# Memory queries as two more units of the gates, and the memory's norm inside u's second half

## The chip, the cores and the metric

The kernel runs on one core of a Trainium2 chip. The metric is the device time of one execution in microseconds (us); the time before is the median of 3 runs.

## The reference, cut to what matters

One decoder layer: a half-step SwiGLU, a mixing block with three branches, a second half-step SwiGLU. The mixing block has one input projection, whose columns feed everything in it:

```python
h = rmsnorm(x, mix_norm)                 # x: 1024 tokens x 1024
z = h @ w_in                             # [u | v | c_q | c_kv | k_rope | q_mem | gate_A | gate_B | gate_C]
u, v = gelu(z_u), gelu(z_v)              # 512 wide each
y_a = spatial_gating(u, v, ...)          # u * (tril(W_s) layernorm(v) + b) in chunks of 128
y_b = mla(...)                           # causal attention with low-rank q and kv
def memory_attention(q_m, mem, mem_norm, w_kv, q_norm, k_norm):     # y_c: 4 heads of 128
    q = rmsnorm(q_m.reshape(B, S, 4, 128), q_norm)
    kv = rmsnorm(mem, mem_norm) @ w_kv                              # mem: 256 x 1024
    k = rmsnorm(kv[..., :512].reshape(B, 256, 4, 128), k_norm)
    v = kv[..., 512:].reshape(B, 256, 4, 128)
    p = softmax(einsum('bshd,bmhd->bhsm', q, k) * 128 ** -0.5)
    return einsum('bhsm,bmhd->bshd', p, v).reshape(B, S, 512)
gates = sigmoid(z_gates + b_gate)        # 3 x 1024
merged = sum(gates[i] * (y_i @ w_branch_i))
x = x + merged @ w_out
```

All is float32.

## The kernel before

**Products.** A float32 product is made of three matmuls of rounded parts (`mm3`, L141): high by high, high by low, low by high. So every operand has a high part (a cast, on ACT, L127) and a low part (a subtraction on DVE, L128). `split_gain` (L135) does both with a gain per partition (L136 on ACT, L137 on DVE). Matmuls are issued one by one in a fixed order; each engine works through its own list, and a scheduler that lays out the program before it runs decides how the lists of neighbouring steps are interleaved.

**Stages.** First feed-forward, 0 to about 690 us; gates, about 690 to 905; then `mixer` (L939): latents and q, k, v of the attention (to about 1020), spatial gate `sgu` (L600, to about 1098), the memory stage `mem_kv` (L669) and `mem_attention` (L715) to about 1250, branch C, the causal attention with branch B, and the output projection; last the second feed-forward.

**Gates.** `Gates.run` (L1486) computes the 24 column tiles (128 wide) of the gates as 12 units of `Seven`: two column tiles by all tokens are cut in 2 x 2 blocks and computed with seven block products instead of eight. A unit is 7 products x 4 tiles of the inner dimension x 3 = 84 matmuls of 512 columns, where the ordinary way takes 96; DVE adds the products up. `emit` (L1472) puts a sigmoid on each half tile and stores the tile to DRAM, feature by token, where the branches fetch it.

**Spatial gate.** `gelu_rows` (L588) computes four row tiles of u for one half of the tokens: for each of eight inner tiles d, four row tiles, 96 matmuls in all, then four gelus on ACT. The first half accumulates in two `mm` slots (each is two banks of the accumulation memory), the second in four `bank`s. Then for each of eight groups one mixing product and one step on DVE that adds the bias and multiplies by u (L643), and 16 transposes of the result with their splits.

**Memory stage.** `branches` (L542) makes branch A as a generator of 16 steps, each of 12 matmuls (column tile by token half) and one multiplication by the gate on DVE (L955, `sink_a`). The memory stage draws on it as filler: `fill(n)` and `F`. `mem_kv` loads mem, squares and sums it, takes the root, makes the norm's scale by two transposes, applies it (`norm_put`, L397: one step on DVE, one cast, one split for each of eight tiles of 256), then computes K, normalises its heads, computes V and transposes K. `mem_attention` loads w_qm; its step R computes one tile of 128 query rows the ordinary way (`zrow`, L403; 24 matmuls), and every second R normalises two tiles (`head_norm`, L653). S transposes one tile of queries (4 transposes), computes its scores against the four heads (12 matmuls of 256 columns into an `mm` slot, of which there are two), takes the maximum (the gain is negated, so a minimum, L746), four exponentials with their sums (L751), and the division (L755, L756). T transposes the probabilities of a tile, V multiplies those of two tiles with the values. The order of R, S, T, V and F is written out in a list at the end of the function.

**Buffers.** Weights arrive in `raw`, a ring of three buffers of 512 KB (L76), and their parts lie in `wide` (five each, L79). SP issues all DMAs in one list, so a load that waits for its buffer holds back those behind it.

## Time and profile before

| | us |
|---|---|
| median of 3 runs | 2202.14 (2200.33 to 2203.34) |
| the profiled execution | 2201.71 |
| its span in the trace | 2200.0 |
| PE busy in the span | 2183.1 (99%) |
| DVE busy | 1548.5 (70%) |
| ACT busy | 896.6 (41%) |
| mean granted clock of TensorE | 0.998 |

The profiled execution's own time is the span and 1.7 us around it. Busy shares are means over stages with different limits, so a stage is read in its own window. In the rows of the views, PE is TensorE's matmuls, PEld its weight loads, DVE VectorE, ACT ScalarE, POOL GpSimd, SP the queue that issues DMAs. Since matmuls are pipelined, the duration of one (0.39 us for 512 columns) is longer than the time from the start of one to the start of the next.

### The profile page before, as it was taken

The page shows a single profiled execution, that of the slowest core. Times are in us where ns is not written, and L with a number is a line of the kernel's source. Part 1 is how long each engine was busy: PE and PEld are TensorE (multiplying, and loading weights), DVE is VectorE, ACT ScalarE, POOL GpSimd, SP SyncE. Part 2 cuts the span into 40 slices and gives each one's busy share as a digit, 9 for nine tenths or more (in the row PEclk, how much of TensorE's full clock was granted, in tenths as well). Part 3 has the DMA queues.
Part 4 walks back from the last instruction along what each step waited for, and adds up shares of the span by engine and source line. Part 5 has one row for each costly group of instructions (what it writes and reads, how often), then busy time and mean ns, then how long its engine had stood idle before and what let it go on. Part 6 is the DMA issues. An engine that isn't in the chain of part 4 may idle for free.

```text
span 2200.0 us, 27606 instructions
## 1 busy us (share of the span) xinstructions
PE 2183.1 (99%) x10304; PEld 1822.2 (83%) x10304; DVE 1548.5 (70%) x2408; ACT 896.6 (41%) x1501; POOL 258.0 (12%) x253
## 2 busy tenths in 40 slices
PE   8999999999999999999999999999999999999999
PEld 5888888888887888898888889988888888888887
DVE  7966666579889555467466769885886666657884
ACT  5432222343455333444244459843432222224332
POOL 2011112100000000022000221140011111210000
PEclk9999999999999999999999999999999999999999
DMA  4242333385432333225151541094033333338443
GB/s 145 82 138 102 101 101 115 123 313 168 135 118 96 125 106 125 94 91 173 50 195 58 212 181 39 21 329 168 29 122 101 98 110 101 115 114 300 170 130 105
DMA packets 113063, 285.93 MB, mean 130 GB/s; under 512 B 13344, under 2 KB 21664, under 8 KB 112800
## 3 DMA queue, kind: packets, MB, share of 16 engines
q1 hardware_dynamic: 112928, 284.16, 38.0%
q8 instruction: 81, 1.33, 0.3%
q14 instruction: 54, 0.44, 0.1%
HBM read 201.80 MB, written 82.31 MB: 129 GB/s over the span
## 4 chain that ended last, share of the span: by engine, by line
PE 92%; DVE 4%; ACT 1%; DMA 1%; issue 1%; POOL 0%; SPq 0%; ACTq 0%; POOLq 0%
PE bank L144 13%; PE bank L146 13%; PE bank L145 13%; PE one L144 13%; PE one L146 13%; PE one L145 13%; PE mm L146 3%; PE mm L144 3%; PE mm L145 3%; PE bank L879 1%; PE bank L415 1%; DMA w<-in_ffn_w_gu_dram 1%; PE bank L894 1%; PE bank L895 1%; DVE wlo L133 1%
## 5 line engine op out<-in xcount | busy, mean ns | idle before, releaser
L132 ACT CAST whi<-x 128x1024 fp32r<-128x1024 f32 (+1 forms) x189 | 179.6, 952 | 472.9 <-PE one L145 206.9
L1283 DVE TENSOR_TENSOR t<-t,one 128x512 f32<-128x512 f32 x178 | 122.3, 687 | 225.7 <-PE one L146 225.6
L144 PE MATMUL bank<-h,whi 128*128 128x512 f32 x644 | 250.8, 390 | 0.0
L145 PE MATMUL bank<-h,whi 128*128 128x512 f32 x644 | 250.7, 389 | 0.0
L146 PE MATMUL bank<-h,wlo 128*128 128x512 f32 x644 | 250.5, 389 | 0.0
L133 DVE TENSOR_TENSOR wlo<-x,whi 128x1024 fp32r<-128x1024 f32 (+1 forms) x189 | 226.2, 1199 | 29.1 <-ACT whi L132 29.0
L144 PE MATMUL one<-h,whi 128*128 128x512 f32 x476 | 187.1, 393 | 0.0
L146 PE MATMUL one<-h,wlo 128*128 128x512 f32 x476 | 186.2, 391 | 0.0
L145 PE MATMUL one<-h,whi 128*128 128x512 f32 x476 | 186.2, 391 | 0.0
L1674 POOL TENSOR_TENSOR raw<-raw 128x512 f32<-128x512 f32 x38 | 63.0, 1658 | 791.7 <-DVE raw L1529 791.7
L128 DVE TENSOR_TENSOR wlo<-w,whi 128x1024 fp32r<-128x1024 f32 (+1 forms) x108 | 110.1, 1033 | 63.5 <-ACT whi L127 63.3
L127 ACT CAST whi<-w 128x1024 fp32r<-128x1024 f32 (+1 forms) x108 | 95.1, 899 | 145.0 <-PE one L145 60.9
L144 PE MATMUL one<-w,whi 128*128 128x512 f32 x392 | 152.5, 389 | 0.0
L145 PE MATMUL one<-w,whi 128*128 128x512 f32 x392 | 152.5, 389 | 0.0
L146 PE MATMUL one<-w,wlo 128*128 128x512 f32 x392 | 152.5, 389 | 0.0
L146 PEld LDWEIGHTS bank<-h,wlo 128*128 128x128 f32 x644 | 120.9, 188 | 25.1
L145 PEld LDWEIGHTS bank<-h,whi 128*128 128x128 f32 x644 | 120.9, 188 | 25.0
L144 PEld LDWEIGHTS bank<-h,whi 128*128 128x128 f32 x644 | 120.9, 188 | 24.7
L144 PE MATMUL bank<-whi 128*128 128x512 f32 x352 | 136.9, 389 | 0.0
L145 PE MATMUL bank<-wlo,whi 128*128 128x512 f32 x352 | 136.9, 389 | 0.0
L146 PE MATMUL bank<-whi,wlo 128*128 128x512 f32 x352 | 136.9, 389 | 0.0
L128 DVE TENSOR_TENSOR wlo<-h,whi 128x512 fp32r<-128x512 f32 x130 | 88.1, 713 | 26.0 <-ACT whi L127 26.0
(382 smaller groups left out, 5054.7 us busy)
## 6 DMA issues: line engine op xcount, KB each, us to landing
x<-in_ffn_w_gu_dram SPq DMA_DIRECT2D x78, 512.0 KB, 5.2
w<-tdt SPq DMA_DIRECT2D x40, 512.0 KB, 4.8
tdb<-raw SPq DMA_DIRECT2D x64, 256.0 KB, 2.1
h<-in_ffn_w_down_dram SPq DMA_DIRECT2D x64, 256.0 KB, 6.0
w<-tdb SPq DMA_DIRECT2D x30, 512.0 KB, 4.7
tdt<-w SPq DMA_DIRECT2D x48, 256.0 KB, 2.1
gate<-raw SPq DMA_DIRECT2D x23, 512.0 KB, 2.6
tdt<-raw SPq DMA_DIRECT2D x40, 256.0 KB, 2.8
```

What stands on the lines that cost most here:

```text
L127: self.nc.scalar.copy(hi, src)
L128: return (eng or self.nc.vector).tensor_tensor(lo, src, hi.bitcast(F32), op=ALU.subtract)
L132: self.nc.scalar.copy(hi, src)
L133: return lambda: self.nc.vector.tensor_tensor(lo, src, hi.bitcast(F32), op=ALU.subtract)
L144: mmul(out, s[0], m[0], start=first, stop=False, **kw)
L145: mmul(out, s[0], m[1], start=False, stop=False, **kw)
L146: self.last = mmul(out, s[1], m[0], start=False, stop=last, **kw)
L415: nc.tensor.transpose(b[:m, k * P:(k + 1) * P], s, self.ident)
L879: nc.tensor.transpose(b[:, at:at + P], prs[t][:, kk * P:(kk + 1) * P], self.ident)
L894: nc.tensor.matmul(o, w, pt[0], start=n == 0, stop=False)
L1283: return self.nc.vector.tensor_tensor(out, x, y, op=ALU.add)
L1674: sub = lambda d, x, y: (eng or nc.gpsimd).tensor_tensor(d, x, y, op=ALU.subtract)
```

## The change

The columns of q_mem leave the ordinary product and are appended to the weights of the gates: 28 column tiles instead of 24, 14 units instead of 12 (`ZB`). The four new tiles are copied instead of passed through a sigmoid, and stored to DRAM as gate24 to gate27: they are the queries of one head each, not normalised, feature by token, so that they need no transposes. u is computed as before.

Inside u's second half, the memory's norm is computed (`mem_norm`): its loads, squares and sums ahead of the half, the token sums ahead of inner tile 4 and the scale and `norm_put` ahead of inner tile 6 (`amid` in `gelu_rows`). Behind the 96 matmuls, `mem_queries` fetches the four query tiles into `raw`, squares them (eight ACT steps on 64 x 1024), splits them with the gain (ACT and DVE on 128 x 1024) and adds the squares up by pairs on POOL. After the V product 16 matmuls with a 128 x 2 selector (`pick`) make the sums of squares per token and head, and `rms` their roots r.

The query's norm is no longer applied to the queries: the minimum of the scores is multiplied by r (one more small DVE step for each tile), and the exponential takes -r as its scale. Probabilities have three buffers. The values of two tiles go into two `bank`s, not into an `mm` slot. The order of S, T, V and F is a new one, without R, with ten F instead of eight; `mem_kv` takes five steps of branch A instead of eight.

```diff
+ZQ = 3 * DT
+ZB = ZQ + MH
...
-    def gelu_rows(self, dst, h, w, pairs):
+    def gelu_rows(self, dst, h, w, pairs, amid={}):
 
 
         gelu = lambda d, x: self.nc.scalar.activation(d, x, ACT.Gelu)
         ps = [self.mm() for _ in range(2)] if pairs else [self.bank() for _ in range(4)]
         for d in range(DT):
+            then = amid[d]() if d in amid else None
             for i in range(4):
                 b = ps[i // 2][:, i % 2] if pairs else ps[i]
-                self.mm3(b, tuple(x[:, i * P:(i + 1) * P] for x in h[d]), w[d], d == 0, d == DT - 1)
+                first = self.mm3(b, tuple(x[:, i * P:(i + 1) * P] for x in h[d]), w[d], d == 0, d == DT - 1)
+                if then:
+                    self.after(first, then)
+                then = None
...
-                self.gelu_rows(u, h[hf], w, hf == 0)
+                if hf:
+                    mem = self.mem_norm()
+                    next(mem)
+                self.gelu_rows(
+                    u, h[hf], w, hf == 0, {4: lambda: next(mem), 6: lambda: next(mem)} if hf else {})
+                if hf:
+                    queries = self.mem_queries()
+                    next(queries)
...
+    def mem_norm(self):
+
+
+        nc, a = self.nc, self.a
+        views = lambda ts: [t[:, i].rearrange("p (c m) -> p c m", m=ML)[:, c]
+                            for t in ts for i in range(2) for c in range(2)]
+        x4 = [self.h4() for _ in range(2)]
+        x = views(x4)
+        for n, t in enumerate(x4):
+            nc.sync.dma_start(
+                t.rearrange("p a (b m) -> p (a b) m", b=2), a["mem"][:, 4 * n:4 * n + 4])
+        acc = None
+        for n in range(4):
+            acc = self.norm_feed(acc, x4[n // 2][:, n % 2], 512)
+        nc.vector.tensor_tensor(acc[:, :ML], acc[:, :ML], acc[:, ML:], op=ALU.add)
+        yield
+        room = lambda: self.mm()[:, 0]
+        ss = self.token_sums(acc[:, :ML], late=True, bank=room)
+        last = self.final
+        r = self.rms(ss, ML // P, D)
+        yield last
+        scale = self.norm_scale(r, late=True, bank=room)
+        last = self.final
+        hi, lo = (views([self.h4(F32R) for _ in range(2)]) for _ in range(2))
+        for c in range(DT):
+            self.norm_put(hi[c], lo[c], x[c], self.g_mem[:, c:c + 1], scale)
+        yield last
+        yield hi, lo
...
+        fill(3)
+        ps = product(self.load(a["mem_w_kv"][0]))
+        w = self.load(a["mem_w_kv"][1])
+        x = p.tile([P, 2, MH, MD], F32, name="m_k")
+        self.head_norm(x, [ps[:, 0], ps[:, 1]])
+        fill(2)
+        ps = product(w)
+        amid()
...
+    def mem_queries(self):
+
+
+        nc = self.nc
+        gq = self.stat("m_gq", 1)
+        nc.gpsimd.tensor_scalar(gq, self.mq_g, -MD ** -0.5, None, op0=ALU.mult)
+        qt, ss = [], []
+        for pair in range(MH // 2):
+            sq = [self.wide(n).bitcast(F32) for n in ("whi", "wlo")]
+            for o in range(2):
+                q = self.raw()
+                nc.sync.dma_start(q, self.z[ZQ + 2 * pair + o].rearrange("p a w -> p (a w)"))
+                qt.append(self.split_pair(self.h4))
+                for n, t in enumerate(sq):
                     nc.scalar.activation(
-                        pr[:, hh], sc[:, hh], ACT.Exp, bias=mx[:, hh:hh + 1], scale=-1.0,
-                        accum_out=sm[:, hh:hh + 1])
-                rs = self.stat("m_rs", MH)
-                nc.vector.reciprocal(rs, sm)
-                nc.vector.tensor_tensor(pr, pr, rs.unsqueeze(2).to_broadcast([P, MH, ML]), op=ALU.mult)
-                out.append(pr)
-
-            def turn(i, k):
-                if k == 0:
-                    pt = [tuple(self.wide(n).rearrange("p (h q) -> p h q", h=MH) for n in ("whi", "wlo")) for _ in range(2)]
-                    st[i] = st[i][1], pt
-                prs, pt = st[i]
-                for m in range(2):
-                    self.to_feature4(
-                        tuple(t[:, :, k * P:(k + 1) * P] for t in pt[m]),
-                        [prs[k][:, hh, m * P:(m + 1) * P] for hh in range(MH)])
-
-            def value(i):
-                pt = st.pop(i)[1]
-                o = self.mm().rearrange("p a (b q) -> p (a b) q", b=2)
-                for hh in range(MH):
+                        t[o * P // 2:(o + 1) * P // 2], q[n * P // 2:(n + 1) * P // 2], ACT.Square)
+                self.split_gain(*qt[-1], q, gq)
+            nc.gpsimd.tensor_tensor(sq[0], sq[0], sq[1], op=ALU.add)
+            ss.append(sq[0])
+        yield
+        b = self.bank()[:, :NT * MH]
+        for pair, sq in enumerate(ss):
+            for t in range(NT):
+                at = t * MH + 2 * pair
+                nc.tensor.matmul(b[:, at:at + 2], sq[:, t * P:(t + 1) * P], self.pick, start=True, stop=True)
+        r = self.const.tile([P, NT * MH], F32, name="mq_r")
+        nc.vector.tensor_copy(r, self.rms(b, NT * MH, MD))
+        nr = self.const.tile([P, NT * MH], F32, name="mq_nr")
+        nc.gpsimd.tensor_scalar(nr, r, -1.0, None, op0=ALU.mult)
+        yield qt, r, nr
...
+            mx = self.stat("m_mx", MH)
+            nc.vector.tensor_reduce(mx, sc, axis=AXX, op=ALU.min)
+            nc.vector.tensor_tensor(mx, mx, r[:, at:at + MH], op=ALU.mult)
+            pr = p.tile([P, MH, ML], F32, name="mpr", bufs=3)
+            sm = self.stat("m_sm", MH)
+            for hh in range(MH):
+                nc.scalar.activation(
+                    pr[:, hh], sc[:, hh], ACT.Exp, bias=mx[:, hh:hh + 1], scale=nr[:, at + hh:at + hh + 1],
+                    accum_out=sm[:, hh:hh + 1])
...
+                o = self.bank().rearrange("p (b q) -> p b q", b=2)
+                for hh in (2 * pair, 2 * pair + 1):
                     for m in range(2):
                         s = tuple(t[:, m, hh * MD:(hh + 1) * MD] for t in vv)
-                        self.mm3(o[:, hh], s, tuple(t[:, hh] for t in pt[m]), m == 0, m == 1)
...
-            for f, *x in ((R, 0, 0), (R, 0, 1), (R, 1, 0), (R, 1, 1), (S, 0, 0), (R, 2, 0), (S, 0, 1), (R, 2, 1),
-                          (S, 1, 0), (R, 3, 0), (S, 1, 1), (R, 3, 1)):
-                f(*x)
...
-            for f, *x in ((T, 0, 0), (F,), (S, 2, 0), (T, 0, 1), (F,), (S, 2, 1), (V, 0), (T, 1, 0), (F,), (S, 3, 0),
-                          (T, 1, 1), (F,), (S, 3, 1), (V, 1), (T, 2, 0), (F,), (T, 2, 1), (F,), (V, 2), (T, 3, 0),
-                          (F,), (T, 3, 1), (F,), (V, 3)):
-                f(*x)
+        for f, *x in (
+                (S, 0, 0), (F,), (S, 0, 1), (F,), (T, 0, 0), (S, 1, 0), (F,), (T, 0, 1), (S, 1, 1), (F,),
+                (V, 0), (T, 1, 0), (S, 2, 0), (F,), (T, 1, 1), (S, 2, 1), (F,), (V, 1), (T, 2, 0), (S, 3, 0), (F,),
+                (T, 2, 1), (S, 3, 1), (F,), (V, 2), (T, 3, 0), (F,), (T, 3, 1), (F,), (V, 3)):
+            f(*x)
...
-        self.nc.scalar.activation(d, ps, ACT.Sigmoid, bias=k.b_gate[:, n:n + 1])
+        if n < ZQ:
+            self.nc.scalar.activation(d, ps, ACT.Sigmoid, bias=k.b_gate[:, n:n + 1])
+        elif row is None:
+            self.nc.scalar.copy(d, ps)
...
+    w = np.concatenate([w[:, at:], w_qm], 1).reshape(2, 4, P, ZB // 2, 2, P).transpose(3, 2, 4, 0, 1, 5)
```

Three places show how the instructions move. First SP, which issues the DMAs, from the gate vectors' loads on; before:

```order
L194 DMA ln_g<-in_sg_ln_g_dram 128x512
L194 DMA ln_b<-in_sg_ln_b_dram 128x512
L93 DMA raw<-in_w_branch_dram 128x512 x5
L93 DMA raw<-in_mem_w_kv_dram 128x1024 x3
L572 DMA x_10110<-gate_3239 128x1024
L677 DMA m_x<-in_mem_dram 128x2048
```

and after (gate_3251 to gate_3254 are the four query tiles, h_8715 and h_8716 hold mem):

```order
L198 DMA ln_g<-in_sg_ln_g_dram 128x512
L198 DMA ln_b<-in_sg_ln_b_dram 128x512
L761 DMA raw<-gate_3251 128x1024
L761 DMA raw<-gate_3252 128x1024
L761 DMA raw<-gate_3253 128x1024
L699 DMA h_8715<-in_mem_dram 128x1024
L699 DMA h_8716<-in_mem_dram 128x1024
L564 DMA t<-gate_3227 128x512
L564 DMA t<-gate_3228 128x512
L564 DMA t<-gate_3229 128x512
L761 DMA raw<-gate_3254 128x1024
L582 DMA x_10038<-gate_3243 128x1024
```

The first branch weights stood directly behind the gate vectors; now the queries and mem stand ahead of them, and the fourth query ahead of them by itself, since the ring has three buffers.

Second DVE, from the end of u's second half to branch A; before (x_8275 to x_8282 are the mixed tiles' parts):

```order
L128 TENSOR_TENSOR wlo<-raw,whi 128x512 x3
L643 SCALAR_TENSOR_TENSOR u<-bank,c_sg_b,u 128x4x64 x3
L128 TENSOR_TENSOR wlo<-raw,whi 128x512
L643 SCALAR_TENSOR_TENSOR u<-bank,c_sg_b,u 128x4x64 x5
L128 TENSOR_TENSOR x_8276<-bank,x_8275 128x512
L128 TENSOR_TENSOR x_8278<-bank,x_8277 128x512
L128 TENSOR_TENSOR x_8280<-bank,x_8279 128x512
L128 TENSOR_TENSOR x_8282<-bank,x_8281 128x512
L955 TENSOR_TENSOR t<-t,bank 128x512
```

and after (h_8715 and h_8716 are mem, h_8829 and h_8830 its low parts, h_8890, h_8898, h_8909 and h_8917 the low parts of the four queries, x_8538 to x_8544 the mixed tiles):

```order
L131 TENSOR_TENSOR h_8829<-h_8715,h_8827 128x256 x4
L131 TENSOR_TENSOR h_8830<-h_8716,h_8828 128x256 x3
L140 SCALAR_TENSOR_TENSOR h_8890<-raw,m_gq,h_8889 128x1024
L131 TENSOR_TENSOR h_8830<-h_8716,h_8828 128x256
L664 SCALAR_TENSOR_TENSOR u<-bank,c_sg_b,u 128x4x64 x4
L140 SCALAR_TENSOR_TENSOR h_8898<-raw,m_gq,h_8897 128x1024
L664 SCALAR_TENSOR_TENSOR u<-bank,c_sg_b,u 128x4x64 x2
L140 SCALAR_TENSOR_TENSOR h_8909<-raw,m_gq,h_8908 128x1024
L664 SCALAR_TENSOR_TENSOR u<-bank,c_sg_b,u 128x4x64 x2
L140 SCALAR_TENSOR_TENSOR h_8917<-raw,m_gq,h_8916 128x1024
L131 TENSOR_TENSOR x_8538<-bank,x_8537 128x512
L131 TENSOR_TENSOR x_8540<-bank,x_8539 128x512
```

The memory's splits and the first query's gain split now stand ahead of the mixing steps, two more gain splits between them, and the fourth query's ahead of the mixed tiles' splits; the first wlo is branch A's first weight, three steps further down. The eight steps of L409 (`norm_put`) stand directly above.

Third the softmax's start, DVE; before, at the first tile of scores:

```order
L667 TENSOR_TENSOR mq<-mq,rs_y 128x1024
L663 TENSOR_REDUCE hn_ss<-t 128x4
L746 TENSOR_REDUCE m_mx<-mm 128x4
L137 SCALAR_TENSOR_TENSOR mq_lo<-bank,m_gq,mq_hi 128x512
L755 RECIPROCAL m_rs<-m_sm 128x4
L756 TENSOR_TENSOR mpr<-mpr,m_rs 128x1024
```

and after:

```order
L1002 TENSOR_TENSOR t<-t,bank 128x512
L796 TENSOR_REDUCE m_mx<-mm 128x4 x2
L797 TENSOR_TENSOR m_mx<-m_mx,mq_r 128x4 x2
L805 RECIPROCAL m_rs<-m_sm 128x4
L806 TENSOR_TENSOR mpr<-mpr,m_rs 128x1024
L796 TENSOR_REDUCE m_mx<-mm 128x4
L805 RECIPROCAL m_rs<-m_sm 128x4
L797 TENSOR_TENSOR m_mx<-m_mx,mq_r 128x4
L806 TENSOR_TENSOR mpr<-mpr,m_rs 128x1024
```

Between the first two tiles of scores stood the norm and the gain splits of queries; now the first two reductions and the two products with r follow one another, ahead of the first division. On PE the second and the third tile of scores stand behind one another, and the first transposes of probabilities behind them, ahead of the next step of branch A (x_8537 is an operand of branch A):

```order
L147 MATMUL mm<-mk_hi,h_8916 128x256
L148 MATMUL mm<-mk_lo,h_8916 128x256
L149 MATMUL mm<-mk_hi,h_8917 128x256
L844 MATMUL bank<-ident,mpr 128x128 x8
L147 MATMUL bank<-x_8537,whi 128x512
L148 MATMUL bank<-x_8538,whi 128x512
L149 MATMUL bank<-x_8537,wlo 128x512
```

Before, some two dozen matmuls of the next query rows stood between two tiles of scores (whi and wlo are parts of w_qm here, h_5142 and h_5143 of the rows):

```order
L145 MATMUL mm<-mk_lo,mq_hi 128x256
L146 MATMUL mm<-mk_hi,mq_lo 128x256
L415 MATMUL bank<-ident,mq 128x128
L144 MATMUL bank<-whi,h_5142 128x512
L145 MATMUL bank<-wlo,h_5142 128x512
L146 MATMUL bank<-whi,h_5143 128x512
L144 MATMUL bank<-whi,h_5142 128x512
```

So the scores have lost what stood between them, and the branch steps stand behind transposes.

More of the change, by code (lines that the diff above doesn't have):

```diff
@@ L650, in sgu @@
                     )
-        return yt
+        return yt, next(mem), queries
     def head_norm(self, x, ps):
@@ L672, in mem_kv @@
+    def mem_kv(self, p, mt, fill, amid):
+        nc, a = self.nc, self.a
         kt = tuple(p.tile([P, MH, ML], F32R, name=n) for n in ("mk_hi", "mk_lo"))
         vv = tuple(p.tile([P, 2, MH * MD], F32R, name=n) for n in ("mv_hi", "mv_lo"))
[L674 to L712 removed]
@@ L773, in value @@
                     for m in range(2):
                         s = tuple(t[:, m, hh * MD:(hh + 1) * MD] for t in vv)
-                        self.mm3(o[:, hh], s, tuple(t[:, hh] for t in pt[m]), m == 0, m == 1)
-                for hh in range(MH):
-                    self.split(*(t[:, 2 * i * P:2 * (i + 1) * P] for t in yt[hh]), o[:, hh])
-            R, S, T, V = rows, scores, turn, value
-            F = lambda: next(filler, None)
-            for f, *x in ((R, 0, 0), (R, 0, 1), (R, 1, 0), (R, 1, 1), (S, 0, 0), (R, 2, 0), (S, 0, 1), (R, 2, 1),
-                          (S, 1, 0), (R, 3, 0), (S, 1, 1), (R, 3, 1)):
-                f(*x)
@@ new lines, in mem_attention @@
+        S, T, V = scores, turn, value
+        F = lambda: next(filler, None)
+        yt = [self.split_pair(self.h4) for _ in range(MH)]
+        for f, *x in (
[3 more added lines that the diff above has]
+            f(*x)
@@ L1460, in __init__ @@
         super().__init__(k, w, pool, norm)
-        self.z = [k.dram.tile([P, 2, 512], F32, name=f"gate{i}") for i in range(3 * DT)]
+        self.z = [k.dram.tile([P, 2, 512], F32, name=f"gate{i}") for i in range(ZB)]
         self.o, self.w0 = {}, {}
```

140 lines of the change are left out of this document (60 added, 80 removed).

## The prediction

> **What bounds the kernel now.** I read the page first: its busy times, and the chain of work that ended last.
>
> ```profile
> PE 2183.1 (99%) x10304; PEld 1822.2 (83%) x10304; DVE 1548.5 (70%) x2408; ACT 896.6 (41%) x1501; POOL 258.0 (12%) x253
> PE 92%; DVE 4%; ACT 1%; DMA 1%; issue 1%; POOL 0%; SPq 0%; ACTq 0%; POOLq 0%
> ```
>
> PE is busy for nearly the whole span and carries nine tenths of the chain, so a matmul removed is time gained, as long as PE finds its next operand ready. The question is therefore what PE waits for now. The waits of PE in the stretch that the change rewrites (1040 to 1300 us: the end of the spatial gate, the memory stage, branch C) are three:
>
> ```profile
> PE mm L144 <- DVE a_mx L857: 1.0, 1, 1.0
> PE mm L146 <- DVE m_lo L128: 0.8, 1, 0.8
> PE bank L144 <- DVE u L643: 0.6, 2, 0.4
> ```
>
> Only the second belongs to the memory stage: the K product waits for the normalised memory. The windows show the work rates. Their columns are PE, PEld, DVE, ACT and POOL busy us with counts, then the granted clock and DMA.
>
> ```profile
> 100.00:600.00 500.00, 500.00 (x2207) 414.01 (x2207) 359.09 (x503) 165.90 (x230) 65.05 (x36) 1.00 0.43 145
> 760.00:800.00 40.00, 40.00 (x178) 33.10 (x178) 20.89 (x27) 14.05 (x18) 0.00 (x0) 1.00 0.35 116
> 1150.00:1175.00 25.00, 25.00 (x122) 20.93 (x121) 10.56 (x29) 6.56 (x12) 0.00 (x0) 1.00 0.07 23
> 1200.00:1225.00 25.00, 25.00 (x166) 22.65 (x165) 22.66 (x41) 15.31 (x43) 0.00 (x0) 1.00 0.33 111
> ```
>
> The first row holds almost only 512-wide matmuls: 500 / 2207 = 0.227 us from start to start. The second is the gates (half of DVE is free), the third the query rows of today (PE long work, DVE 42% busy), the fourth the softmax stage (DVE 91% busy). Today PE is never idle in either of the last two: the query rows are the filler that covers the softmax.
>
> **The change, part by part.**
>
> *PE's work.* The rows of the query product and the transposes of the queries go:
>
> ```profile
> L144 PE MATMUL bank<-whi,h 128*128 128x512 f32 x64 | 25.4, 396 | 0.0
> L415 PE MATMUL bank<-ident,mq 128*128 128x128 f32 x32 | 5.4, 272 | 0.0
> 1069.76 0.82 PE L415 MATMUL bank<-ident,u 128*128 128x128 f32 x6
> 1093.16 0.28 PE L146 MATMUL bank<-v_hi,x 128*128 128x256 f32 x1
> 1093.28 0.28 PE L144 MATMUL bank<-v_hi,x 128*128 128x256 f32 x1
> ```
>
> The first row is one of three such lines, 192 matmuls: 192 x 0.227 = 43.6 us less. A transpose costs (0.82 - 0.27) / 5 = 0.11 from start to start: 32 x 0.11 = 3.5 less. Two more units of the gates add 2 x 84 matmuls: 38.1 more. The 16 pick matmuls (128x2) stand in no row; the smallest are the transposes, so I take 0.11 each, 1.8 more, between 0.5 and 3.6 (16 x 0.227). Sum: -7.2 us. In the gates the added work has the cover of the second window: DVE needs 20.9 of 40 us there, so each unit stays bound by PE; its weights and the four stores of 512 KB add to DMA engines that are 35% busy there. The three memsets of pick cost a tenth of a microsecond each on POOL at the start, where PE waits for the identity anyway:
>
> ```profile
> 0.94 0.10 POOL L203 MEMSET ones<- 128x1 f32 x1
> PE bank L211 <- POOL ident masks.py:199: 1.5, 1, 1.5
> ```
>
> The m_lo wait goes, since the memory is normalised before branch A begins: -0.8. Together -8.0.
>
> *The tail of u's second half.* This is the first new cost. Now:
>
> ```profile
> 1070.67 0.50 PE L144 MATMUL bank<-whi,h 128*128 128x512 f32 x1
> 1091.41 1.96 ACT L591 ACTIVATE u<-bank 128x512 f32<-128x512 f32 x3
> 1093.40 1.27 DVE L643 SCALAR_TENSOR_TENSOR u<-bank,c_sg_b,u 128x256 f32<-128x256 f32 x3 [4.04 <-ACT u L591]
> 1095.18 2.04 DVE L643 SCALAR_TENSOR_TENSOR u<-bank,c_sg_b,u 128x256 f32<-128x256 f32 x5
> 1098.18 0.50 PE L144 MATMUL bank<-x,whi 128*128 128x512 f32 x1
> 1118.66 3.21 DVE L399 SCALAR_TENSOR_TENSOR m_x<-m_x,c_mem_norm,bank 128x256 f32<-128x256 f32 x8
> 1121.80 1.42 DVE L128 TENSOR_TENSOR m_lo<-m_x,m_hi 128x256 fp32r<-128x256 f32 x4
> ```
>
> From the half's first matmul (t = 0) the last gelu ends at +22.7, the eight mixing steps of DVE at +26.6, and branch A starts at +27.5. Afterwards the norm's scale is on PE behind 77 of the 96 matmuls, so DVE's eight norm steps (3.2) run from about +18.5 to +21.7, seven splits (0.34 each, with ACT's casts between) to +24.1, and then, ahead of the mixing, the first query's 1024-wide gain split. ACT puts the casts and that query's gain between the gelus, so the last gelu ends at +25.5. Prices of the 1024-wide steps:
>
> ```profile
> L137 DVE SCALAR_TENSOR_TENSOR mq_lo<-bank,m_gq,mq_hi 128x512 fp32r<-128x512 f32 x8 | 6.0, 745 | 0.0
> L756 DVE TENSOR_TENSOR h<-h,m_rs 128x1024 f32<-128x1024 f32 x6 | 7.3, 1224 | 0.1
> L127 ACT CAST mv_hi<-mm 128x1024 fp32r<-128x1024 f32 x1 | 1.0, 1014 | 1.6 <-PE mm L146 1.6
> raw<-in_mem_w_kv_dram SPq DMA_DIRECT2D x8, 512.0 KB, 3.5
> raw<-in_w_branch_dram SPq DMA_DIRECT2D x5, 256.0 KB, 2.5
> L128 DVE TENSOR_TENSOR wlo<-raw,whi 128x512 fp32r<-128x512 f32 x34 | 22.3, 684 | 5.4 <-ACT whi L127 5.3
> ```
>
> DVE's gain split lies between 1.2 and 2 x 0.745 = 1.5: I take 1.35, in the middle. ACT's square and its gain I put at the cast of the same width, 1.0 (0.7 and 1.4 are half a doubling to either side). The fourth query needs a raw buffer, and the first comes free when DVE's first gain split ends, +25.4. On SP this load stands ahead of a gate tile and of branch A's first three weight loads, which wait behind it and for the same three buffers (today they are loaded before u begins). Then one line: load 3.5 (+28.9), two squares and the gain 3.1 (+32.0), DVE's split 1.35 (+33.4), and only behind it on DVE the split of the first mixed tile and three more steps, 0.68 each (+36.1), the last of them branch A's first low weight. PE needs that for its fifth matmul there. The mixing itself, eight steps of 0.39 with two gain splits between, ends at +31.3 and is hidden behind this line. Without any of it branch A would start at +28.1 (0.6 us of new sums and transposes): 36.1 - 28.1 - 4 x 0.227 = **+7.1**. Bounds: 4.9, if the load lands in 2.5, the gain splits take 1.2 and ACT's steps 0.7; 8.6, if they take 1.5 and 1.4.
>
> *The softmax stage.* The query rows are gone from it; ten steps of branch A (12 matmuls of 0.227 each) are the fillers instead of eight. From the first K transpose: 8 x 0.11, two branch steps 24 x 0.227 = 5.4, and two tiles of scores, 24 x 0.12 (the start-to-start of the 256-wide rows above) = 2.9, make 9.2. The third tile needs the first one's mm slot, so all its exponentials:
>
> ```profile
> L746 DVE TENSOR_REDUCE m_mx<-mm 128x4 f32<-128x1024 f32 x8 | 9.8, 1222 | 1.0 <-PE mm L146 0.7
> 1175.12 1.28 ACT L751 ACT_TABLE_LOAD   x1
> 1176.42 0.48 ACT L751 ACTIVATE mpr<-mm,m_mx 128x256 f32<-128x256 f32 x1
> 1178.14 0.21 ACT L751 ACTIVATION_READ_ACCUMULATOR mpr<-mm,m_mx 128x1 f32 x1
> ```
>
> DVE does both tiles' reductions before the first product with the norm: 9.2 + 0.3 + 1.2 + 0.2 = 10.9. Then the table load, which the new order leaves behind the same wait (1.28), and four exponentials, 1178.35 - 1176.42 = 1.93: 14.1. PE waits 14.1 - 9.2 = 4.9 us; 3.6 if the table is loaded early. No filler stands in between, because the next branch step is ordered behind the first transposes of probabilities. Today this table load passes beside query rows. Later in the stage DVE, 91% busy in the fourth window already, has a branch step and two more sinks to pass between the low parts of the transposed probabilities, and by the new order four branch steps stand on PE behind such a part: behind the first of tile 3 (0.75), a sink (0.5), the first of tile 4 (1.3) and the split of the second value pair (0.6), 3.15 together, each the 0.68 of a split or the 1.2 of a product that DVE has in front. I take 4.25, between the two table cases, and 3.15: **+7.4**; ends 3.6 (early table, nothing later) and 11.2 (late table, twice as much later).
>
> One clock effect is visible at the start of this trace:
>
> ```profile
> PE bank L373 <- POOL t L1128: 2.9, 1, 2.9
> 37.00:40.30 3.30, 0.43 (x3) 0.01 (x1) 3.30 (x2) 0.55 (x2) 3.16 (x2) 1.00 0.01 2
> 40.80:47.65 6.85, 6.85 (x22) 5.58 (x22) 4.66 (x14) 1.05 (x1) 0.00 (x0) 0.50 0.00 0
> ```
>
> After a PE wait of 2.9 us the granted clock is 0.50 for 6.85 us, which costs about half of that, 3.4 us. The new waits are of that length. The Trainium skill (TensorE: Matmul & The Clock Gate, "Part 1: The HAM clock gate") says that the array falls to half clock after an idle window of about 3.4 us, and that this window runs free. By that rule the 2.9 us wait should trip only with thin work around it, as here, and the softmax gap of 3.6 to 4.9 us would trip only if it fills a window. I leave it out of the sum and make it a rival.
>
> *Sum*: -8.0 + 7.1 + 7.4 = +6.5. The profiled execution took 2201.7 us (span 2200.0, and 1.7 around it), 0.4 below the median 2202.1. Forecast: 2202.1 + 6.5, about **2208.5**.
>
> **The rivals.**
>
> *The waits stay covered (the other side).* If the fourth query's chain is shorter than I run it and the fillers are there when PE needs them, only the work counts: 2202 - 8 = 2194. For it: DVE and ACT are at 70% and 41% over the whole, and PE's waits in this stretch are 2.4 us today. Against it: the buffer ring and the two mm slots are hard orders. It decides where the two places come to under 3.6 us in sum (8.0 less the 4.4 that can be told apart).
>
> *One of the two shows.* 2202.1 - 8.0 + 7.2 = 2201.3, no change. For it: each has its own cause, and in either one step on the other side of a neighbour would break the line.
>
> *Half clock after a gap.* Both waits and one stretch of 6.85 us at 0.50: 2208.5 + 3.4 = 2211.9; two: 2215.3. For it: the row at 40.80. Against it: the tail's wait is broken up by mixing matmuls, and shorter waits (1.0 here) leave the clock at 1.00.
>
> That the change does less than it says can't be: the order of instructions has 40 matmuls fewer (192 + 32 - 168 - 16).
>
> **How the numbers follow.** Both waits 0.42 (own range 2202.5 to 2213.8, both ends low or both high), one of them 0.22, none 0.18, half clock 0.18. A measurement of this kernel can tell about 0.2%, 4.4 us, from no change: 2197.7 to 2206.5. Faster: the case of no waits and 0.07 of the case of one, 0.25. Same: the rest of the case of one and 0.07 of my own, 0.22. Slower: 0.53. The range leaves out the best part of the first rival and the doubled half clock: 2194.5 to 2215.
>
> **What would show it.** Right: in the profile after, PE waits of about 7 us in sum just ahead of branch A, on mixed u and on a weight's low part, with the fourth query's load issued near the last gelu; a PE gap of 3.5 to 5 us ahead of the third tile of scores, beside a table load and exponentials; gates longer by 38 us; no m_lo wait. Wrong: PE idle under 3 us between the second half of u and branch C (then the first rival holds), a wait in the gates or in the K and V products, which I cost at nothing, or a clock below 1.00 at either gap.

## The result

| | median, us | runs |
|---|---|---|
| before | 2201.2 (2198.7 to 2203.3) | 4 |
| the changed kernel | 2214.6 (2213.8 to 2215.5) | 4 |

The changed kernel is slower: ratio 1.0061, 95% interval 1.0044 to 1.0079. In the 13 and the 27 runs of the kernel before that were made beside the experiments its median is 2199.5 and 2199.7, so the loss is between 13 and 15 us; 6.5 were forecast.

The profiled execution of the changed kernel took 2213.9 us (span 2212.1). Page: busy times and chain.

```profile
PE 2182.9 (99%) x10280; PEld 1821.0 (82%) x10280; DVE 1548.5 (70%) x2386; ACT 902.0 (41%) x1489; POOL 262.8 (12%) x259
PE 89%; DVE 6%; ACT 2%; issue 1%; DMA 1%; POOL 0%; SPq 0%; ACTq 0%; DVEq 0%; POOLq 0%
```

PE has fewer matmuls and is called busy as long as before, and its share of the chain went from 92% to 89%, for DVE and ACT. What PE waits for between 1040 and 1330 us, its five longest (the same stretch of work as before; a row ends in the sum in us, the number of waits and the longest):

```profile
PE mm L147 <- ACT mpr L801: 5.1, 1, 5.1
PE bank L147 <- ACT whi L130: 3.4, 1, 3.4
PE bank L147 <- DVE wlo L131: 2.2, 2, 1.3
PE bank L147 <- ACT u L601: 1.1, 2, 0.9
PE bank L147 <- DVE h L131: 1.0, 2, 0.7
```

The m_lo wait is gone. In its place stand the softmax's exponentials (first row), the high part of branch A's first weight (second), the gelus of u's second half (fourth) and low parts in the softmax stage (third and fifth; the two waits of the third row are at 1218.33 and 1231.29, ahead of branch steps).

The change is read best from one point of the work to another, since the two profiled executions differ by 2.9 us before the change is reached at all (the 2001st matmul starts at 474.74 before and at 471.88 after). From the first matmul of u's second half to the first of the attention, windows of before and of after:

```profile
1070.67:1287.35 216.68, 215.38 (x1111) 183.49 (x1111) 134.96 (x266) 86.14 (x209) 22.68 (x21) 1.00 0.47 166
```

```profile
1105.93:1298.83 192.90, 178.73 (x918) 152.00 (x919) 112.89 (x215) 74.59 (x177) 25.61 (x23) 0.97 0.50 176
```

This stretch is 23.8 us shorter, where the two new units cost 38.1 in the gates (2 x 84 x 0.227, and the latents indeed start 35.27 later, 38.1 with the 2.86 of the start added): +14.3. Idle time of PE grew from 1.3 to 14.2 us, and the granted clock is 0.97 on the mean. Where the idle time lies: the tail of u (before, then after), the way to the K product, and the softmax behind its first wait, of after:

```profile
1070.67:1098.18 27.51, 27.05 (x137) 22.83 (x137) 8.39 (x17) 6.84 (x13) 0.00 (x0) 1.00 0.22 68
```

```profile
1105.93:1141.40 35.47, 30.00 (x142) 24.89 (x142) 19.04 (x43) 15.03 (x26) 2.35 (x1) 0.95 0.15 45
1141.40:1162.22 20.82, 20.48 (x92) 16.83 (x92) 9.39 (x15) 5.12 (x11) 0.00 (x0) 0.92 0.48 163
1203.00:1255.08 52.08, 48.80 (x314) 43.49 (x312) 39.66 (x69) 29.71 (x85) 2.01 (x3) 1.00 0.36 118
```

That is 5.5 + 0.3 in the tail against 0.5 before, and 3.3 late in the softmax; its first wait, 5.1, follows below.

The tail, DVE's rows; t = 0 is at 1105.93:

```profile
1130.16 1.28 DVE L140 SCALAR_TENSOR_TENSOR h<-raw,m_gq,h 128x1024 fp32r<-128x1024 f32 x1
1131.69 1.65 DVE L664 SCALAR_TENSOR_TENSOR u<-bank,c_sg_b,u 128x256 f32<-128x256 f32 x4
1136.43 0.87 DVE L664 SCALAR_TENSOR_TENSOR u<-bank,c_sg_b,u 128x256 f32<-128x256 f32 x2
1138.35 2.30 DVE L140 SCALAR_TENSOR_TENSOR h<-raw,m_gq,h 128x1024 fp32r<-128x1024 f32 x1 [1.04 <-ACT h L139]
1140.57 1.27 DVE L131 TENSOR_TENSOR x<-bank,x 128x512 fp32r<-128x512 f32 x2
```

SP, ACT, DVE and PE beside it (the fourth query's load, the first branch weights, the first weight's high and low part, branch A's first matmul and its first with a low weight):

```profile
1131.46 0.32 SPq L761 DMA_DIRECT2D raw<-gate  x1
1135.38 5.63 SPq L96 DMA_DIRECT2D raw<-in_w_branch_dram  x3
1140.81 0.62 ACT L130 CAST whi<-raw 128x512 fp32r<-128x512 f32 x1 [1.05 <-DMA raw<-in_w_branch_dram]
1142.37 0.67 DVE L131 TENSOR_TENSOR wlo<-raw,whi 128x512 fp32r<-128x512 f32 x1
1141.47 0.50 PE L147 MATMUL bank<-x,whi 128*128 128x512 f32 x1 [3.42 <-ACT whi L130]
1143.50 0.63 PE L149 MATMUL bank<-x,wlo 128*128 128x512 f32 x1
```

The first gain split ends at +25.5, the fourth query's load is issued then, its gain split starts at +32.4, the low weight is there at +37.1 and used at +37.6. These steps are the forecast ones (+25.4, +32.0, +36.1). The last part is about 1 us longer: the fourth gain split took 2.30 us, not 1.28 as the other three.

But PE did not wait for that low weight. Its wait of 3.42 us ahead of branch A ended with the first weight's high part, on a second line that the forecast does not have: the weight's load stands on SP behind the fourth query's and a gate tile's, is issued at 1135.38 and lands at 1140.8, after 5.4 us (the forecast's row had 2.5), and ACT's cast follows. The forecast line was only just behind: DVE's split of the first mixed tile (it starts at 1140.57, the second of its kind right behind it) ended at about 1141.2, so PE would have waited nearly as long without the load.

The softmax's start, rows of PE, DVE and ACT (the last matmul of the second tile, the first of the third; the two reductions; the table load):

```profile
1191.79 0.28 PE L149 MATMUL mm<-mk_hi,h 128*128 128x256 f32 x1
1197.14 0.58 PE L147 MATMUL mm<-mk_hi,h 128*128 128x256 f32 x1 [5.07 <-ACT mpr L801]
1190.79 2.54 DVE L796 TENSOR_REDUCE m_mx<-mm 128x4 f32<-128x1024 f32 x2 [0.63 <-PE mm L149]
1193.50 1.28 ACT L801 ACT_TABLE_LOAD   x1 [8.91 <-DVE m_mx L797]
```

The wait is 5.07 us, with the table load in it. And the clock, windows on the edges of its steps:

```profile
1132.24:1135.66 3.42, 3.42 (x15) 3.29 (x16) 3.42 (x7) 1.58 (x2) 0.00 (x0) 0.50 0.53 153
1135.66:1142.48 6.82, 2.55 (x17) 1.64 (x16) 5.78 (x8) 5.68 (x9) 2.35 (x1) 1.00 0.59 189
1142.48:1145.90 3.42, 3.42 (x8) 2.72 (x9) 2.37 (x4) 0.62 (x1) 0.00 (x0) 0.50 0.50 178
1192.00:1197.10 5.10, 0.07 (x1) 0.00 (x0) 1.44 (x4) 3.59 (x10) 0.00 (x0) 1.00 0.19 56
1197.10:1200.50 3.40, 3.36 (x15) 3.36 (x16) 1.79 (x3) 2.18 (x8) 0.00 (x0) 0.50 0.00 0
```

Three stretches at half clock, each 3.41 us, so up to about 5.1 us lost in all: two in the tail, one right behind the softmax's wait. Eight matmuls start in the third row, where 15 would at full clock.

### The profile page after: what moved, and what is told of

Its sections match the earlier page's. It is cut to its first block, busy times and chain, and to the rows that moved or that the text cites. A ratio compares the mean times of both kernels' runs of the same rounds, so it can differ in the third digit from the quotient of the medians.

```text
span 2212.1 us, 27569 instructions
## 1 busy us (share of the span) xinstructions
PE 2182.9 (99%) x10280; PEld 1821.0 (82%) x10280; DVE 1548.5 (70%) x2386; ACT 902.0 (41%) x1489; POOL 262.8 (12%) x259
## 3 DMA queue, kind: packets, MB, share of 16 engines
q1 hardware_dynamic: 114224, 288.36, 37.6%
## 4 chain that ended last, share of the span: by engine, by line
PE 89%; DVE 6%; ACT 2%; issue 1%; DMA 1%; POOL 0%; SPq 0%; ACTq 0%; DVEq 0%; POOLq 0%
PE one L147 13%; PE one L148 13%; PE one L149 13%; PE bank L147 13%; PE bank L148 12%; PE bank L149 12%; PE mm L147 2%; PE mm L148 2%; PE mm L149 2%; PE bank L926 1%; PE bank L941 1%; PE bank L942 1%; PE bank L425 1%; DVE wlo L136 1%; DVE wlo L131 1%
## 5 line engine op out<-in xcount | busy, mean ns | idle before, releaser
L135 ACT CAST whi<-x 128x1024 fp32r<-128x1024 f32 (+1 forms) x195 | 185.5, 953 | 489.7 <-PE one L148 215.5
L147 PE MATMUL bank<-h,whi 128*128 128x512 f32 x660 | 257.1, 390 | 0.0
L148 PE MATMUL bank<-h,whi 128*128 128x512 f32 x660 | 256.9, 389 | 0.0
L149 PE MATMUL bank<-h,wlo 128*128 128x512 f32 x660 | 256.8, 389 | 0.0
L136 DVE TENSOR_TENSOR wlo<-x,whi 128x1024 fp32r<-128x1024 f32 (+1 forms) x195 | 233.0, 1196 | 30.5 <-ACT whi L135 30.4
L147 PE MATMUL one<-h,whi 128*128 128x512 f32 x492 | 193.1, 393 | 0.0
L148 PE MATMUL one<-h,whi 128*128 128x512 f32 x492 | 192.0, 390 | 0.0
L149 PE MATMUL one<-h,wlo 128*128 128x512 f32 x492 | 192.0, 390 | 0.0
L147 PE MATMUL one<-w,whi 128*128 128x512 f32 x408 | 158.7, 389 | 0.0
L148 PE MATMUL one<-w,whi 128*128 128x512 f32 x408 | 158.7, 389 | 0.0
L149 PE MATMUL one<-w,wlo 128*128 128x512 f32 x408 | 158.7, 389 | 0.0
L147 PEld LDWEIGHTS bank<-h,whi 128*128 128x128 f32 x660 | 123.9, 188 | 25.9 <-DVE h L131 0.4
L148 PEld LDWEIGHTS bank<-h,whi 128*128 128x128 f32 x660 | 123.9, 188 | 25.6
L148 PEld LDWEIGHTS one<-h,whi 128*128 128x128 f32 x492 | 92.8, 189 | 19.3 <-issue 0.2
```

The lines of the kernel that those rows point to most:

```text
L135: self.nc.scalar.copy(hi, src)
L136: return lambda: self.nc.vector.tensor_tensor(lo, src, hi.bitcast(F32), op=ALU.subtract)
L147: i = mmul(out, s[0], m[0], start=first, stop=False, **kw)
L148: mmul(out, s[0], m[1], start=False, stop=False, **kw)
L149: self.last = mmul(out, s[1], m[0], start=False, stop=last, **kw)
```

## The experiments

The theory: the tail costs what the line of the queries costs (buffer ring, gain splits ahead of the mixed tiles), the softmax what the missing filler costs, and half clock comes on top. The rivals: the memory's norm makes the tail; the softmax stage is bound by DVE and ACT whatever the order; a wait removed comes back elsewhere. "Half to attention" is the stretch of the two windows above, in each profiled execution: 216.7 us before, 192.9 after. The ratios are to runs of the kernel before beside each experiment. The changed kernel was not run again beside them, so a difference from its 2214.6 carries the 1.5 to 1.7 us by which the median of the kernel before moved; the stretch leaves out what differs at the start of the program.

| kernel | median, us | half to attention, us |
|---|---|---|
| own_room | 2217.2 | 194.6 |
| q_early | 2207.0 | 183.1 |
| hold | 2206.6 | 184.5 |
| early_table | 2214.8 | 193.1 |
| hold1 | 2208.8 | 187.5 |
| both | 2200.1 | 176.6 |
| both_late | 2198.4 | 176.5 |
| both_norm | 2196.2 | 175.2 |

**own_room.** The fourth query in a tile of its own.

```diff
-                q = self.raw()
+                q = self.h4().rearrange("p a w -> p (a w)") if pair and o else self.raw()
```

> The changed kernel with the fourth query loaded into a tile of its own instead of the ring of three weight buffers; the order of DVE stays (gain splits between the mixing steps and ahead of the mixed tiles). If the tail of u's second half costs what it does because the load waits for the ring (theory), the fourth gain split starts right behind the last mixing step (at +31.4 after the half's first matmul instead of +32.4) and without the POOL addition beside it, branch A's first low weight is there at +35.2 instead of +37.1: 2 us less than the changed kernel's 2214.6, with one stretch of half clock less perhaps 3.7 less. If the memory's norm alone delays the tail (rival), no change.

2217.2 us, ratio to before 1.0076 (1.0061 to 1.0091). It did not do what it was to do. SP's list in its trace:

```profile
1133.38 0.33 SPq L96 DMA_DIRECT2D raw<-in_w_branch_dram  x1
1133.80 0.38 SPq L761 DMA_DIRECT2D h<-gate  x1
```

The scheduler put the load behind the first branch weight, which itself waits for the ring, so it still started only when the first gain split had freed a buffer. Its stretch is 1.7 us longer than the changed kernel's, as much as one more step at half clock costs, and its tail has one more:

```profile
1138.74:1148.98 10.24, 6.83 (x19) 5.19 (x20) 6.97 (x10) 5.46 (x9) 2.35 (x1) 0.50 0.52 171
```

Three steps at half clock in one piece, over the start of branch A. The first branch weight, on the other hand, was loaded earlier here (issued 25.5 us after the half's first matmul, not 29.4), and PE waited about as long as in the changed kernel, now for the mixed tile's low part, which stands behind the fourth gain split:

```profile
1144.27 0.80 PE L147 MATMUL bank<-x,whi 128*128 128x512 f32 x1 [3.28 <-DVE x L131]
```

So the forecast line holds branch A up by itself when the weight is early. The share of the ring alone stays open.

**q_early.** The queries ahead of u's second half.

```diff
-                self.gelu_rows(
-                    u, h[hf], w, hf == 0, {4: lambda: next(mem), 6: lambda: next(mem)} if hf else {})
-                if hf:
                     queries = self.mem_queries()
                     next(queries)
+                self.gelu_rows(
+                    u, h[hf], w, hf == 0, {4: lambda: next(mem), 6: lambda: next(mem)} if hf else {})
```

> The changed kernel with the four queries fetched, squared and split ahead of u's second half, where DVE was busy 1.6 of 10 us, instead of behind its 96 matmuls; the memory's norm stays inside that half. Theory (the line of the queries makes the tail): PE idle in the tail falls from 5.8 us to about 1.5, the two stretches of half clock there go, the first branch weights arrive before the tail, and the time falls by 5 to 8 us, to 2207 to 2210. Rival (the norm's steps among the gelus and on DVE make the tail): less than 2 us, 2213 or above.

2207.0 us (1.0031, 1.0020 to 1.0042), 7.6 less than the changed kernel. The window of the whole tail, first matmul of the half to first of branch A:

```profile
1107.65:1137.48 29.83, 28.45 (x143) 23.59 (x143) 18.29 (x43) 11.69 (x23) 2.40 (x1) 1.00 0.22 72
```

The tail takes 29.8 us instead of 35.5, PE is idle for 1.4, the clock stays at 1.00, and neither branch weight is waited for. With the norm untouched, the rival has only what is left: 29.8 against 27.5 before, 0.6 of it new sums and transposes. The edit moves the load, the squares and the splits together, so it shows the line of the queries as the cause, not which link of it. The waits show a new one, in the first half, where two gain splits now stand ahead of the mixing:

```profile
PE bank L147 <- DVE u L663: 2.8, 3, 1.9
```

**hold.** Branch steps between the second and the third tile of scores.

```diff
+            if j == 0 and self.hold:
+                self.after(i, self.hold)
...
-                (S, 0, 0), (F,), (S, 0, 1), (F,), (T, 0, 0), (S, 1, 0), (F,), (T, 0, 1), (S, 1, 1), (F,),
+                (F,), (S, 0, 0), (S, 0, 1), (H,), (F,), (S, 1, 0), (T, 0, 0), (T, 0, 1), (S, 1, 1), (F,),
```

H is F with its first matmul bound behind the last one of the scores.

> The changed kernel with two steps of branch A (24 matmuls, 5.4 us) held behind the second tile of scores, ahead of the third, and one step ahead of the first. Theory (the third tile waits for the exponentials of the first because nothing stands between): the wait of 5.1 us and the half clock behind it (1.7 us) go, later waits grow by 1 to 2: 2208 to 2210. Rival (the stage is bound by DVE and ACT whatever the order): the wait comes back later in the stage in full, 2213 to 2215.

2206.6 us (1.0031, 1.0020 to 1.0042), 8.0 less. The waits of its softmax stage, all of them (the a_mx wait belongs to the attention and was there before):

```profile
PE mm L149 <- DVE a_mx L914: 1.0, 1, 1.0
PE bank L149 <- DVE h L133: 0.8, 2, 0.4
PE bank L854 <- DVE mpr L810: 0.6, 1, 0.6
```

The long wait is gone and did not come back: the later waits did not grow, though both I and the rival expected it, but fell from 3.3 to 1.4 us. From K's first transpose to the attention the kernel takes 107.5 us instead of 116.2; its tail, which the edit does not touch, had 10.2 us at half clock in this execution instead of 6.8. The stage has the DVE and ACT time it needs; it lacked two branch steps in the right place.

**early_table.** The table loaded ahead.

```diff
+        nc.scalar.activation(self.stat("m_ex", 1), r[:, :1], ACT.Exp)
```

> The changed kernel with one exponential of a single column (its result is not used) ahead of the softmax, so that ACT loads its table before the first scores are there. The wait ahead of the third tile of scores falls from 5.1 to 3.8 us, the time by 1.3 us to about 2213.3; if the half clock behind the wait goes too, by 3. If the table load passed beside something else anyway, no change.

The wait fell as expected, and the time did not: 2214.8 us (1.0067, 1.0050 to 1.0084). Its row of the waits, and its window behind the wait:

```profile
PE mm L147 <- ACT mpr L802: 3.8, 1, 3.8
```

```profile
1197.85:1204.68 6.83, 5.54 (x23) 5.35 (x24) 3.98 (x7) 5.09 (x20) 0.00 (x0) 0.50 0.02 6
```

The half clock lasted two steps instead of one; what the shorter wait gave, the clock took. Its tail, too, had 10.2 us at half clock instead of 6.8.

**hold1.** One held step instead of two.

> The changed kernel with one branch step held between the second and the third tile of scores, not two: the wait of 5.1 us should shrink by 12 x 0.227 = 2.7 to about 2.4 us. If half clock follows only a window of 3.41 us that is nearly empty of matmuls, there is none after this wait, and the time is 2.4 above the kernel with two held steps: about 2209. If half clock follows any wait over 2 us, it stays and the time is 2210 to 2211.

2208.8 us (1.0045, 1.0030 to 1.0061). The wait, and a window around it:

```profile
PE mm L149 <- ACT mpr L805: 2.9, 1, 2.9
```

```profile
1190.00:1200.00 10.00, 7.14 (x42) 5.92 (x41) 6.74 (x12) 8.74 (x25) 0.00 (x0) 1.00 0.24 81
1190.23:1193.65 3.42, 1.65 (x8) 1.03 (x6) 1.58 (x4) 2.54 (x6) 0.00 (x0) 1.00 0.26 98
1193.65:1197.06 3.41, 2.32 (x19) 2.28 (x20) 1.98 (x3) 3.26 (x13) 0.00 (x0) 1.00 0.39 133
```

2.9 us, and the clock stays at 1.00. From K's first transpose to the attention it takes 110.8 us, 3.4 more than hold: the wait, and 0.5 of others. So behind waits of one place, 2.9 us left the clock alone, 3.8 and 5.1 did not. The two last rows are steps of the clock's grid (last section): the wait, 1191.9 to 1194.7, lay across two of them, so neither was empty. What the same wait does inside one step, this run does not show.

**both, both_late, both_norm.** Both edits; then the gain splits kept behind the last split of u's first half on both engines; then the memory's norm two inner tiles earlier.

```diff
-                self.split_gain(*qt[-1], q, gq)
+                for i, j in zip(self.split_gain(*qt[-1], q, gq), (self.hi_last, self.lo_last)):
+                    self.after(i, j)
...
-                    u, h[hf], w, hf == 0, {4: lambda: next(mem), 6: lambda: next(mem)} if hf else {})
+                    u, h[hf], w, hf == 0, {2: lambda: next(mem), 4: lambda: next(mem)} if hf else {})
```

> The queries ahead of u's second half and the two held branch steps together, on top of the changed kernel. If the two places are separate causes, their gains add: from the start of u's second half to the start of the attention 192.9 us in the changed kernel, 183.1 with the early queries, 184.5 with the held steps, so 174.7, and the time is 2214.6 - 9.8 - 8.4, plus about 1 in u's first half: 2197 to 2198, level with or slightly below the kernel before. If one wait only takes the other's place, 2203 or more.

> The kernel of both, with the queries' gain splits kept behind the last split of u's first half on ACT and DVE, since with the early queries DVE's mixing steps of the first half started 1.9 us late. The waits of 2.8 us of PE on the mixing of the first half go: 1 to 2 us less than both, 2195 to 2197, faster than before by 0.1 to 0.2%. If that wait was hidden, the same as both.

> The kernel of both_late, with the memory's token sums ahead of inner tile 2 and its scale ahead of inner tile 4 of u's second half, not 4 and 6, so that ACT's casts are through before the gelus. If the norm still costs something in the tail (rival on the norm), 0.5 to 1.5 us less than both_late; if not, the same.

both: 2200.1 us, ratio 1.0004 (0.9995 to 1.0012). Together the two edits take 14.5 us off the changed kernel, 7.6 and 8.0 alone. It came out 2 above what I expected, half to attention 176.6 instead of 174.7: of the 9.8 us that q_early had gained there, 2.1 lay in the softmax stage (K's transposes to the attention took 114.1 us instead of 116.2, with smaller later waits), and hold removes the same waits. Stage by stage the gains add up to 0.1 us: up to K's transposes both takes 69.1 us as q_early does (76.7 in the changed kernel), from there 107.5 as hold does. So these are two causes. both_late: 2198.4 us (0.9993, 0.9984 to 1.0002), not told from before, with 1.7 less as expected, but above the 2195 to 2197 given for it. both_norm: 2196.2 us, 0.9986 (0.9977 to 0.9995), and 2.2 below both_late, above the range I gave. Its tail and its whole stretch:

```profile
1105.50:1133.88 28.38, 27.92 (x142) 23.48 (x142) 21.97 (x46) 16.06 (x27) 2.39 (x1) 1.00 0.33 103
```

```profile
1105.50:1280.67 175.17, 173.22 (x919) 147.99 (x920) 113.43 (x215) 74.47 (x177) 25.64 (x23) 1.00 0.55 194
```

The tail went from 29.8 to 28.4, so about 1.4 of the gain is the norm's work done earlier (that it is the casts between the gelus is argued, not shown). In the profiled executions 0.7 of the rest lies ahead of the 2001st matmul, which the edit does not touch. This version is the change as it could have been: 18.4 us faster than as it was, 3.5 faster than before, with its idle time at 2.0 us.

## Why the prediction was right, and why too small

**Direction.** The forecast's likeliest case, both waits, is what happened, at the two places that it named; in the softmax by the chain that it named, in the tail by that chain and a second one beside it. The time, 2214.6, is above the likeliest case's own range (2202.5 to 2213.8), and just inside the whole range (2194.5 to 2215), because the rival of the half clock came true on top, at both places.

**PE's work.** The gates' +38.1 is exact. The rest was put at -45.3; the busy time of the stretch fell by 215.4 - 173.2 = 42.2, taken from both_norm, where the clock is whole. Of the difference, 3.1, up to 1.7 is the pick matmuls: 32 rows of the trace for 16 instructions.

```profile
L774 PE MATMUL bank<-pick,whi 128*128 128x2 f32 x32 | 3.8, 238 | 0.0
```

At the 0.11 of the forecast they cost 3.5, not 1.8, inside the bounds of that term but wrong in its count. I could have read it: the two token sums of the memory are counted four times in the trace of before. The other 1.4 are not attributed.

**The tail, +7.1.** PE's idle time from the half's first matmul into the K product is 5.8 us after and 0.5 before, +5.4, and two stretches of half clock add up to 3.4: 8.8. q_early confirms the line of the queries as a whole: it takes it away, and with it 5.7 of the 8.0 us by which the tail had grown. Two steps I did not have. I put the delay on the low weight, for which PE did not wait at all; it waited 3.4 us for the high part, whose load took 5.4 us to land, a line that I had not costed. That the two lines ended within 0.3 us of each other is luck for the forecast. And the fourth gain split was held up by POOL (below), 1.0; an estimate from the rows above is that this cost PE 0.3 of waiting at most, its wait for a mixed tile's low part behind branch A's second matmul, since the high weight came at 1141.4 in any case. The norm's share, which I had only as the delay of the gelus, is about 1.4.

**The softmax, +7.4.** Wait 5.07 (4.25 taken between the two table cases; the late table, 4.9, was the right one), later waits 3.3 (3.15 forecast), half clock 1.7: 10.1. hold shows the cause. The later waits are right in the sum only: four of 1.3, 1.0, 0.7 and 0.3, where I had 0.75, 0.5, 1.3 and 0.6. What I had wrong is that they are a matter of DVE's time: with the two steps moved they fell too.

**The clock.** The failed step of the sum is "I leave it out of the sum and make it a rival": three stretches of 3.41 us at 0.50 cost about 5.1 us in the profiled execution. The prediction named a clock below 1.00 at either gap as a sign of being wrong, and that sign came. My reason against it in the tail, that mixing matmuls break the wait up, was wrong: the clock fell there twice, once behind 13 matmuls in 3.41 us, with no single wait over 1 us among them (windows below). The size is that of one execution: the mean granted clock of the four runs was 0.997, 0.997, 0.995 and 0.994, and the profiled one is among the highest. From 0.997 to 0.994, by the rounded figures, 4 to 9 us more of clock are lost (an estimate, 0.002 to 0.004 of 2213), while the time grew by 1.5 us only; so a step at half clock does not always cost the whole 1.7 us.

**The sum by its measured parts**: 38.1 - 42.2 - 0.8 (m_lo) + 5.4 + 8.4 (PE's idle time) + 5.5 (the busy time that after has over both_norm, the clock in it) = 14.4, against 14.3 measured between the same points. No new wait appeared in the gates (one of 1.6 us was there before) or in the K and V products, which I had costed at nothing.

## What to carry to other kernels

Work that is moved takes its cover with it: the query rows were the filler of the softmax, and when they went to a stage that needs no filler, the scores stood alone; count for each stage what fills it after the move. A load that shares a small ring with the next stage's weights, and work for an engine that the next stage waits for, are better placed where ring and engine are idle: two lines moved ahead of 96 matmuls were worth 7.6 us here, though how much of that is the ring is not shown. Where new waits, in one piece or several, leave PE short of work for some 3 us, put the half clock into the sum: here it was about a third of the loss.

## What the runs showed of the hardware

**Half clock comes in whole steps.** All stretches at 0.50 in these traces, but for a last one that the end of each trace cuts off, last 3.41 us or two or three times that, and within one run all lie on one grid of that step (in the changed kernel 1132.24, 1142.48 and 1197.10 are 3 and 16 steps apart). The Trainium skill (TensorE: Matmul & The Clock Gate, "Part 1: The HAM clock gate") gives a window of 3413 ns that runs free, and a drop after an idle one; the length of the steps agrees. That the number of steps varies for the same kind of wait (one behind 5.1 us, two behind 3.8) fits a grid that runs free, but the runs don't test that by themselves; another reason may be that PE was busy for only 2.13 us of the first of those two steps, against 3.37 in the one behind 5.1 us. The same 2.9 us wait near the start of the program was followed by 6.85 us at half clock in the profiled run of before and by 3.41 in that of after:

```profile
39.98:43.39 3.41, 3.41 (x10) 2.73 (x10) 3.06 (x14) 1.04 (x1) 0.00 (x0) 0.50 0.00 0
```

That alone is 1.7 of the 2.9 us by which the two profiled executions differ at the start.

How empty a step must be can't be read from PE's busy time alone. The steps ahead of the three stretches of the changed kernel, and between them one that no stretch followed (the third row of four; the stretches begin at the ends of the first, second and fourth):

```profile
1128.83:1132.24 3.41, 1.86 (x13) 1.25 (x11) 3.41 (x9) 3.41 (x6) 0.00 (x0) 1.00 0.00 0
1139.07:1142.48 3.41, 0.74 (x2) 0.30 (x3) 3.41 (x5) 2.31 (x5) 0.50 (x1) 1.00 0.30 98
1135.66:1139.07 3.41, 1.81 (x15) 1.34 (x13) 2.37 (x4) 3.37 (x5) 1.86 (x1) 1.00 0.89 280
1193.68:1197.10 3.42, 0.00 (x0) 0.00 (x0) 0.00 (x0) 3.41 (x10) 0.00 (x0) 1.00 0.19 67
```

1.86 us of 3.41 in 13 matmuls lost the clock, 1.81 in 15 (most of them transposes) did not. In the other runs 2.06 us lost it too (hold, 1131.10 to 1134.51), and 1.65 did not (hold1, above). So a step need not be idle here, other than the Trainium skill's rule has it. What counts there stays open.

**A POOL addition holds DVE up.** The fourth gain split (1138.35, 2.30 us) began while POOL added two tiles of squares; the other three took 1.28. It is the same in own_room, early_table, hold and hold1 (2.30 or 2.31, begun beside POOL's addition).

```profile
1137.21 2.35 POOL L767 TENSOR_TENSOR whi<-whi,wlo 128x1024 f32<-128x1024 f32 x1 [51.79 <-ACT wlo L764]
```

POOL was done at 1139.56; 1139.56 - 1138.35 = 1.2, about the 1.0 that the split took longer. In q_early a step of two columns on DVE, 0.16 us otherwise, was caught in the same way:

```profile
1119.44 2.21 DVE L158 TENSOR_SCALAR rs_y<-rms_v 128x2 int32<-128x2 int32 x1
```

It ended at 1121.65, when POOL's addition (from 1119.22, 2.40 us) was through. The Trainium skill (SBUF — State Buffer, "SBUF: two separate sides") has DVE and GpSimd share a port pair that one of them holds for a whole instruction while the other blocks, for a DVE step with two inputs from SBUF or in a two-port mode. The gain split has two such inputs and agrees with it; the two-column step has one, and its mode is not shown.
